# Summing two weight blocks in HBM by an accumulating DMA, and seven products in place of eight in seven more granules

## The chip, the cores and the metric

The kernel runs on one core of a Trainium2 chip. The time is device microseconds of one execution, and the time before is the median of three runs. The core has five engines with a queue each, which go through their instructions in order and wait for each other by semaphores: PE (matrix products), DVE (element-wise), ACT (element-wise and functions), POOL (element-wise, and DMAs of its own) and SP, which here only issues DMAs. The transfers themselves run on 16 DMA engines that all queues share. Weights lie in HBM; PE reads SBUF and writes PSUM, which has eight banks of 128 x 512 f32 words.

## The reference

One decoder layer for 256 tokens of width 2048. The input is normalized and multiplied with one wide matrix, the result is cut into nine parts, two token mixers run side by side, and their outputs are merged by gates and projected:

```python
h = rms_norm(x, norm_g)
q, k, v, z_a, u_b, v_b, z_b, g_a, g_b = jnp.split(h @ w_in, cuts, axis=-1)
q = rms_norm(q.reshape(B, S, N_ATT_HEADS, HEAD_DIM), q_norm_g)
k = rms_norm(k.reshape(B, S, N_ATT_HEADS, HEAD_DIM), k_norm_g)
att = moba_attention(q, k, v)          # causal here: 256 tokens are one block
y_a = (att * jax.nn.silu(z_a)) @ w_proj_a
sgu = spatial_gating(jax.nn.gelu(u_b), jax.nn.gelu(v_b), sgu_norm_g, w_s, b_s)
y_b = (sgu * jax.nn.silu(z_b)) @ w_proj_b
merged = jax.nn.sigmoid(g_a) * y_a + jax.nn.sigmoid(g_b) * y_b
return x + merged @ w_out
```

q, k, v, z_a, u_b, v_b and z_b are 1024 columns wide, g_a and g_b 2048 each. All inputs are f32. The host may lay the inputs out anew; it does no arithmetic.

## The kernel before, in words

*Granules.* The weights are 120 granules of 128 x 2048 words (1 MB), in the order in which they are used: `schedule()` (L50). A "quad" granule holds four 128 x 512 blocks W12, W11, W22, W21, in this order: two blocks of 128 input features (a pair, `kp`, 0 to 7) by two blocks of 512 output columns. Eight pairs make a stage. The stages are q, k, v, za, vb, ub, zb, then four gate blocks g0 to g3, each followed by four "proj" granules of the two projections, then two output blocks. The order of the pairs within a stage is written out by hand (L43 to L46).

*Three matmuls per product.* A product in f32 is split: each operand is cut into a high part (a cast to fp32r) and a low part (the difference), and low x high, high x high and high x low are added (`three`, L285). ACT makes the high parts of the weights, DVE the low parts.

*Eight products or seven.* A direct granule is eight products of a 128 x 128 block of x with a 128 x 512 block of weights, 24 matmuls (`direct`, L294). Some quad granules use seven products instead (`seven`, L308), after Winograd's form of Strassen's method: 21 matmuls. They need sums of weight blocks, T0 = W12 + W11, T1 = W12 + W22, T2 = T0 + W22, T3 = T2 + W21, and four forms of x that are made once (`four_forms`, L269). `strassen(i)` (L105) says which granules: pairs 0 to 3 of every stage but q, and pair 4 of the gate blocks, 52 in all. Three of the seven products go straight into the output banks `L`, the other four into the banks `E`; after the last seven-product granule of a stage `early` (L333) combines `E`, and `final` (L350) adds `L`. The next stage swaps `E` and `L`. The forms of pair 4 are made by `forms_4`, and `halves_4` puts their two parts in a piece of the tiles of x that only q's direct granules read.

*What DVE and ACT do per granule* is in `split` (L128). For a direct granule, one cast and one difference, 2048 wide. For a seven-product granule: the sums T0 and T1 in one instruction (L143, 1024 wide), T2 (L145) and T3 (L146), into a tile `t` that takes one of the five slots of `raw`; a cast and a difference of the three blocks that are used as they are (L152, L155, 1536 wide, `whp`, `wlp`); and two casts and two differences of the four sums (L154, L157, 1024 wide, `th`, `tl`).

*Order.* The loop at L640 goes over the granules. In step i it emits the load of granule i + 3, the split of granule i + 2, the matmuls of granule i, and then what `at(...)` (L569 to L615) put behind that granule: norms, transposes, attention, the functions. For DVE and ACT this order is kept up to granule 8 (`ordered`, L617); behind it a planner orders each engine's queue by its own estimate of times. The slots limit how far the splits run ahead: the tags `wh` and `wl` have three, `whp` three, `wlp` two, `raw` five. A load waits for its slot of `raw` on SP's queue, and what is behind it there waits too. POOL has a few masks and constants, and the power in `rsqrt` (L244) for the norms of q, k and vb.

Of the kernel before, what the change touches and what calls it, by code (L numbers as in the profile page):

```python
# [20 lines left out]
P = 128  # L21
S = 256
# [45 lines left out]
def hybrid_layer_kernel(  # L68
# [18 lines left out]
    psum = ctx.enter_context(tc.tile_pool(name="psum", bufs=1, space=bass.MemoryType.PSUM))  # L87

# [13 lines left out]

    raw, wh, wl, th, tl = {}, {}, {}, {}, {}

    def strassen(i):  # L105
# [22 lines left out]
    def split(i, pieces=1, js=None):  # L128
# [3 lines left out]
        if not strassen(i):  # L132
# [4 lines left out]
            for j in js or range(pieces):  # L137
# [3 lines left out]
        t = wpool.tile([P, WORDS], F32, tag="raw", bufs=5, name=f"t{i}")  # L141
        two = t[:, 0:2 * B].rearrange("p (a n) -> p a n", a=2)
        nc.vector.tensor_tensor(two, r[:, B:3 * B].rearrange("p (a n) -> p a n", a=2),  # L143
                                r[:, None, 0:B].to_broadcast([P, 2, B]), op=ALU.add)
        nc.vector.tensor_tensor(t[:, 2 * B:3 * B], t[:, 0:B], r[:, 2 * B:3 * B], op=ALU.add)  # L145
        nc.vector.tensor_tensor(t[:, 3 * B:], t[:, 2 * B:3 * B], r[:, 3 * B:], op=ALU.add)  # L146
        wh[i] = wpool.tile([P, 3 * B], F32R, tag="whp", bufs=3, name=f"whp{i}")
        wl[i] = wpool.tile([P, 3 * B], F32R, tag="wlp", bufs=2, name=f"wlp{i}")
        th[i] = wpool.tile([P, WORDS], F32R, tag="wh", bufs=3, name=f"th{i}")
        tl[i] = wpool.tile([P, WORDS], F32R, tag="wl", bufs=3, name=f"tl{i}")  # L150
        a, b = slice(0, 2 * B), slice(2 * B, WORDS)
        nc.scalar.copy(wh[i], r[:, B:])  # L152
        for sl in (a, b):
            nc.scalar.copy(th[i][:, sl], t[:, sl])  # L154
        nc.vector.tensor_tensor(wl[i], r[:, B:], f(wh[i]), op=ALU.subtract)  # L155
        for sl in (a, b):
# [604 lines left out]
```

## Time and profile before

| what | us |
|---|---|
| median of three runs (660.52 to 661.25) | 660.79 |
| the profiled execution | 660.26 |
| its span, first to last instruction | 658.5 |
| PE busy, 2980 matmuls and transposes | 650.4 |
| DVE busy, 606 instructions | 606.3 |
| ACT busy, 564 instructions | 427.8 |
| POOL busy, 26 instructions | 25.3 |
| time of the DMA engines taken by SP's queue | 55.4% |

The span counts what the profiler recorded on the engines; the execution's own time is a little longer. A busy time says how long an engine had something in work, so two engines can both be busy nearly all the time; which of them sets the pace is seen only where one waits for the other. "PEld" is the loading of the stationary operand, which overlaps the matmuls. In a timeline a row is the start in us from the span's beginning, the length in us, the engine, the line, the operation and its tiles, and in brackets the idle time before it with what ended it.

### The profile page before, as it was taken

Reading aid. Unit: us, or ns where it says so; the run is one execution under the profiler, and the core shown is the slowest. Engines: PE = TensorE matmul, PEld = TensorE weight load, DVE = VectorE, ACT = ScalarE, POOL = GpSimd, SP = SyncE. Lnnn points to the kernel's source line nnn. Section 1 sums busy time; section 2 is a strip of 40 time slices with the busy share of each in tenths; the row PEclk is TensorE's granted clock in tenths of the full one; section 3 lists DMA queues with packets and bytes.
Section 4 is the critical chain, followed back from the end, with each engine's and each line's share of the span. In section 5 each row is a group of like instructions: output and inputs, shape, how many; then the busy total and the mean of one; then the engine's idle time right before and its main releaser. Section 6 shows DMA issues by size and latency. Waiting matters only on the chain.

```text
span 658.5 us, 7820 instructions
## 1 busy us (share of the span) xinstructions
PE 650.4 (99%) x2980; PEld 538.7 (82%) x2980; DVE 606.3 (92%) x606; ACT 427.8 (65%) x564; POOL 25.3 (4%) x26
## 2 busy tenths in 40 slices
PE   8999999999999999999999999999999999999997
PEld 5888887888888888888888888888888888888886
DVE  5879997999999799999999999899799979998995
ACT  7889779658886589675655755556474546746360
POOL 1002203000000003000000000000000000000000
PEclk9999999999999999999999999999999999999999
DMA  8975643652664456456449436834755483557641
GB/s 312 420 311 209 261 153 129 255 193 86 236 222 161 163 188 219 165 192 230 153 159 351 137 127 264 302 130 190 266 183 192 137 319 130 189 190 282 198 153 64
DMA packets 22213, 135.32 MB, mean 205 GB/s; under 512 B 2464, under 2 KB 3104, under 8 KB 7072
## 3 DMA queue, kind: packets, MB, share of 16 engines
q1 hardware_dynamic: 21024, 132.73, 55.4%
q10 hardware_dynamic: 1152, 2.10, 0.9%
q8 instruction: 23, 0.38, 0.2%
q14 instruction: 14, 0.11, 0.1%
HBM read 132.72 MB, written 2.10 MB: 205 GB/s over the span
## 4 chain that ended last, share of the span: by engine, by line
PE 93%; DVE 3%; POOL 1%; DMA 1%; issue 1%; ACT 0%; SPq 0%; DVEq 0%
PE acc_g L290 16%; PE y L290 13%; PE acc_out L290 9%; PE seven_g L290 8%; PE acc_q L290 6%; PE acc_vb L290 5%; PE acc_za L290 5%; PE acc_ub L290 5%; PE acc_zb L290 5%; PE acc_k L290 4%; PE seven_out L290 3%; PE acc_v L290 2%; PE seven_vb L290 2%; PE seven_zb L290 2%; PE seven_ub L290 2%; PE seven_za L290 2%
## 5 line engine op out<-in xcount | busy, mean ns | idle before, releaser
L126 DVE TENSOR_TENSOR wl<-raw,wh 128x2048 fp32r<-128x2048 f32 (+2 forms) x76 | 156.2, 2062 | 27.7 <-ACT wh L125 27.3
L154 ACT CAST th<-t 128x1024 fp32r<-128x1024 f32 x104 | 107.7, 1055 | 102.0 <-DVE t L146 35.3
L125 ACT CAST wh<-raw 128x2048 fp32r<-128x2048 f32 (+2 forms) x76 | 130.9, 1730 | 60.2 <-issue 25.3
L157 DVE TENSOR_TENSOR tl<-t,th 128x1024 fp32r<-128x1024 f32 x104 | 125.2, 1222 | 2.9 <-ACT th L154 2.9
L155 DVE TENSOR_TENSOR wlp<-raw,whp 128x1536 fp32r<-128x1536 f32 x52 | 91.0, 1750 | 1.2 <-ACT whp L152 1.2
L152 ACT CAST whp<-raw 128x1536 fp32r<-128x1536 f32 x52 | 76.8, 1482 | 23.6 <-DMA raw<-in_w 21.5
L143 DVE TENSOR_TENSOR t<-raw 128x1024 f32<-128x1024 f32 x52 | 63.3, 1218 | 1.8 <-DMA raw<-in_w 1.5
L290 PE MATMUL acc_g<-wh,xul 128*128 128x512 f32 x96 | 37.3, 389 | 0.0
L290 PE MATMUL acc_g<-wh,xuh 128*128 128x512 f32 x96 | 37.3, 389 | 0.0
L290 PE MATMUL acc_g<-wl,xuh 128*128 128x512 f32 x96 | 37.3, 389 | 0.0
L145 DVE TENSOR_TENSOR t<-t,raw 128x512 f32<-128x512 f32 x52 | 36.0, 691 | 0.2
L146 DVE TENSOR_TENSOR t<-t,raw 128x512 f32<-128x512 f32 x52 | 35.6, 685 | 0.4
L290 PE MATMUL acc_q<-wh,xuh 128*128 128x512 f32 x64 | 25.0, 391 | 1.2 <-ACT wh L125 1.2
L290 PE MATMUL acc_q<-wl,xuh 128*128 128x512 f32 x64 | 25.2, 395 | 0.3 <-DVE wl L126 0.2
L290 PE MATMUL y<-wh,zbl 128*128 128x512 f32 x64 | 25.1, 392 | 0.0
L290 PE MATMUL y<-wh,zal 128*128 128x512 f32 x64 | 25.0, 390 | 0.0
L290 PE MATMUL acc_q<-wh,xul 128*128 128x512 f32 x64 | 24.9, 390 | 0.0
L290 PE MATMUL acc_out<-wh,mh 128*128 128x512 f32 x64 | 24.9, 389 | 0.0
L290 PE MATMUL acc_out<-wl,mh 128*128 128x512 f32 x64 | 24.9, 389 | 0.0
L290 PE MATMUL y<-wl,zah 128*128 128x512 f32 x64 | 24.9, 389 | 0.0
L290 PE MATMUL y<-wh,zbh 128*128 128x512 f32 x64 | 24.9, 389 | 0.0
L290 PE MATMUL y<-wl,zbh 128*128 128x512 f32 x64 | 24.9, 389 | 0.0
(496 smaller groups left out, 1582.2 us busy)
## 6 DMA issues: line engine op xcount, KB each, us to landing
raw<-in_w SPq DMA_DIRECT2D x116, 1024.0 KB, 4.8
raw<-in_w SPq DMA_DIRECT2D x7, 512.0 KB, 8.1
xnat<-in_x SPq DMA_DIRECT2D x2, 1024.0 KB, 16.0
xres<-in_x ACTq DMA_DIRECT2D x8, 256.0 KB, 3.9
out<-out_c SPq DMA_DIRECT2D x5, 256.0 KB, 2.5
xt<-in_xT SPq DMA_DIRECT2D x2, 512.0 KB, 8.2
xt<-in_xT SPq DMA_DIRECT2D x3, 256.0 KB, 9.0
raw<-in_w SPq DMA_DIRECT2D x2, 256.0 KB, 4.3
```

The source lines that it names most:

```text
L125: nc.scalar.copy(h, r)
L126: nc.vector.tensor_tensor(l, r, f(h), op=ALU.subtract)
L143: nc.vector.tensor_tensor(two, r[:, B:3 * B].rearrange("p (a n) -> p a n", a=2), r[:, None, 0:B].to_broadcast([P, 2, B]), op=ALU.add)
L145: nc.vector.tensor_tensor(t[:, 2 * B:3 * B], t[:, 0:B], r[:, 2 * B:3 * B], op=ALU.add)
L146: nc.vector.tensor_tensor(t[:, 3 * B:], t[:, 2 * B:3 * B], r[:, 3 * B:], op=ALU.add)
L152: nc.scalar.copy(wh[i], r[:, B:])
L154: nc.scalar.copy(th[i][:, sl], t[:, sl])
L155: nc.vector.tensor_tensor(wl[i], r[:, B:], f(wh[i]), op=ALU.subtract)
L157: nc.vector.tensor_tensor(tl[i][:, sl], t[:, sl], f(th[i][:, sl]), op=ALU.subtract)
L290: nc.tensor.matmul(acc, a, b, start=(start and n == 0), stop=(stop and n == 2))
```

## The change

*The first sum is made in HBM.* A ring of six HBM tiles of 128 x 512 words is added. For each seven-product granule, SP copies its first block (W12) from the weights into a tile of the ring (`pre_copy`, emitted eight granules ahead), and POOL issues a DMA that adds the second block (W11) onto it (`pre_sum`, six granules ahead). The load of such a granule (three ahead, as before) is then two DMAs: the sum from the ring into the first 512 words of `raw`, and the other three blocks as they are.

*Fewer sums on DVE.* `raw` now begins with W12 + W11. T2 is its sum with W22, T1 is T2 - W11, T3 is T2 + W21: three instructions of 512. `raw` as a whole is cut into `wh` and `wl` (2048 wide), the three new sums into `th` and `tl` (1536 wide), with one cast and one difference each.

*More granules with seven products.* Pair 4 in k, v, vb and zb, and pair 5 in g1, g2 and g3: 59 instead of 52. The forms of pair 5 (`forms_5`) have tiles of their own; `halves_4` moves from granule 20 to granule 8. The orders of the pairs change in these stages.

*Slots and order.* `raw` has four slots, `t` one of its own (1536 wide), `wh` and `wl` three for all granules, `th` three, `tl` two. SP's and POOL's queues are now in the order of the program throughout. The masking of the mixing weights (`causal_mix`) moves from stage vb to stage ub; the tile with x's first piece and the vectors is released early, after the vectors are copied.

```diff
+LATE = (5, 6, 0, 1, 2, 3, 4, 7)
+GATE6 = (6, 0, 1, 2, 3, 4, 5, 7)
+FIVE = ("k", "v", "vb", "zb", "g")
+SIX = (1, 2, 3)
...
-        quad(name, 0, MIXED)
+        quad(name, 0, {"k": GATE, "v": LATE, "vb": LATE, "zb": LATE}.get(name, MIXED))
     for c in range(4):
-        quad("g", c, GATE)
+        quad("g", c, GATE6 if c in SIX else GATE)
...
+    queues = {mybir.EngineType.SP, mybir.EngineType.Pool}
+    ctx.enter_context(tc.manual_schedule(engines=queues))
+    ring = [dram.tile([P, B], F32, tag=f"ring{n}", name=f"ring{n}") for n in range(6)]
...
-        return G[i][3] in SK or (G[i][1] == "g" and G[i][3] == 4)
+        name, c, kp = G[i][1:4]
+        return kp in SK or (name in FIVE and kp == 4) or (name == "g" and c in SIX and kp == 5)
...
-        raw[i] = wpool.tile([P, WORDS], F32, tag="raw", bufs=5, name=f"raw{i}")
+        raw[i] = wpool.tile([P, WORDS], F32, tag="raw", bufs=4, name=f"raw{i}")
+
+    def pre_copy(i):
+        if i < NG and strassen(i):
+            pre[i] = ring[len(pre) % len(ring)]
+            nc.sync.dma_start(pre[i], w[i, :, 0:B])
+
+    def pre_sum(i):
+        if i in pre:
+            nc.gpsimd.dma_start(pre[i], w[i, :, B:2 * B], accum_op=ALU.add)
...
+        if i in pre:
+            nc.sync.dma_start(raw[i][:, 0:B], pre[i])
+            load_piece(i, B, WORDS)
+            return
...
-        t = wpool.tile([P, WORDS], F32, tag="raw", bufs=5, name=f"t{i}")
...
+        t = wpool.tile([P, 3 * B], F32, tag="t", bufs=1, name=f"t{i}")
+        wh[i] = wpool.tile([P, WORDS], F32R, tag="wh", bufs=3, name=f"wh{i}")
+        wl[i] = wpool.tile([P, WORDS], F32R, tag="wl", bufs=3, name=f"wl{i}")
+        th[i] = wpool.tile([P, 3 * B], F32R, tag="th", bufs=3, name=f"th{i}")
+        tl[i] = wpool.tile([P, 3 * B], F32R, tag="tl", bufs=2, name=f"tl{i}")
+        T1, T2, T3 = (t[:, a * B:(a + 1) * B] for a in range(3))
+        nc.scalar.copy(wh[i], r)
+        nc.vector.tensor_tensor(T2, r[:, 0:B], r[:, 2 * B:3 * B], op=ALU.add)
+        nc.vector.tensor_tensor(T1, T2, r[:, B:2 * B], op=ALU.subtract)
+        nc.vector.tensor_tensor(T3, T2, r[:, 3 * B:], op=ALU.add)
+        nc.scalar.copy(th[i], t)
+        nc.vector.tensor_tensor(wl[i], r, f(wh[i]), op=ALU.subtract)
+        nc.vector.tensor_tensor(tl[i], t, f(th[i]), op=ALU.subtract)
...
+    def forms_5():
+        Fs = u("F5").rearrange("p (a k t) -> p a k t", a=4, t=P)
+        four_forms(Fs, xt[1][:, 2:4, :])
+        nc.scalar.copy(F5h, Fs)
+        nc.vector.tensor_tensor(F5l, Fs, f(F5h), op=ALU.subtract)
...
+    at(i0 + 4, lambda: nc.scalar.copy(vec, vec0))
     at(i0 + 4, forms_4)
+    at(i0 + 4, forms_5)
...
-    at(i0 + 20, halves_4)
+    at(i0 + 8, halves_4)
...
     at(i0 + 0, turn_z, "za", None)
+    at(i0 + 0, causal_mix)
...
         if i:
             load(i + 3)
+        if i >= 1:
+            pre_copy(i + 8)
+            pre_sum(i + 6)
         split(i + 2, 2 if i < 2 else 1)
```

More of the change, by code (lines that the diff above doesn't have):

```diff
@@ L87, in hybrid_layer_kernel @@
     psum = ctx.enter_context(tc.tile_pool(name="psum", bufs=1, space=bass.MemoryType.PSUM))
+    dram = ctx.enter_context(tc.tile_pool(name="dram", bufs=1, space=bass.MemoryType.DRAM))
     def slot(dtype, name):
@@ L140, in split @@
             return
-        t = wpool.tile([P, WORDS], F32, tag="raw", bufs=5, name=f"t{i}")
[L142 to L156, printed above, removed]
-            nc.vector.tensor_tensor(tl[i][:, sl], t[:, sl], f(th[i][:, sl]), op=ALU.subtract)
+        t = wpool.tile([P, 3 * B], F32, tag="t", bufs=1, name=f"t{i}")
[11 more added lines that the diff above has]
+        nc.vector.tensor_tensor(tl[i], t, f(th[i]), op=ALU.subtract)
     X = {}
@@ L162, in heads @@
         return ap.rearrange("p (h d) -> p h d", d=P)
-    xv = const.tile([P, NVEC + S], F32, name="xv")
-    vec = xv[:, 0:NVEC]
+    xv = u("xv")
+    vec0 = xv[:, 0:NVEC]
+    vec = const.tile([P, NVEC], F32, name="vec")
     xt = [slot(F32, f"xt{i}").rearrange("p (k t) -> p k t", t=S) for i in range(2)]
@@ L175, in hybrid_layer_kernel @@
     new_raw(0)
-    nc.sync.dma_start(xv, xT[:, 0:NVEC + S])
+    nc.sync.dma_start(xv[:, 0:NVEC + S], xT[:, 0:NVEC + S])
     load_piece(0, 0, B)
@@ L207, in split_x @@
         for j in js or range(2):
-            src = xv[:, NVEC:] if kp + j == 0 else xt[i][:, a + j, :]
-            nc.scalar.activation(xt[i][:, a + j, :], src, AF.Copy, scale=vec[:, 2 * kp + j:2 * kp + j + 1])
+            src = xv[:, NVEC:NVEC + S] if kp + j == 0 else xt[i][:, a + j, :]
+            nc.scalar.activation(xt[i][:, a + j, :], src, AF.Copy, scale=vec0[:, 2 * kp + j:2 * kp + j + 1])
         sl = slice(a + js[0], a + js[0] + 1) if js else slice(a, a + 2)
@@ L217, in hybrid_layer_kernel @@
     mhalf = const.tile([P, 8], F32, name="mhalf")
-    nc.gpsimd.memset(mhalf, -0.5)
-    ninf = const.tile([P, 1], F32, name="ninf")
+    nc.gpsimd.memset(mhalf[:, 0:4], -0.5)
+    ninf = mhalf[:, 4:5]
     nc.gpsimd.memset(ninf, NEG_INF)
@@ L233, in load_mix, with causal_mix @@
             nc.sync.dma_start(t, wsT[:, 4 * c:4 * c + 4, :])
+        nc.sync.dma_start(gain, bass.AP(tensor=sg.tensor, offset=sg.offset, ap=[[0, P], [1, P]]))
+    def causal_mix():
+        for c in range(2):
+            t = heads(X["ws"][c])
             nc.gpsimd.affine_select(out=t, in_=t, pattern=[[0, 4], [1, P]], base=0,
                                     channel_multiplier=-1, compare_op=ALU.is_ge, fill=0.0)
-        nc.sync.dma_start(gain, bass.AP(tensor=sg.tensor, offset=sg.offset, ap=[[0, P], [1, P]]))
     rstd = const.tile([P, 2], F32, name="rstd")
@@ L258, in forms_4 @@
         X["F4"] = Fs[:, :, 0]
+    F5h, F5l = (const.tile([P, B], F32R, name=n).rearrange("p (a k t) -> p a k t", a=4, t=P) for n in ("F5h", "F5l"))
+    def forms_5():
[3 more added lines that the diff above has]
+        nc.vector.tensor_tensor(F5l, Fs, f(F5h), op=ALU.subtract)
     def halves_4():
@@ L317, in Fm @@
                 return spare(hs[0])[:, n], spare(ls[0])[:, n]
+            if kp == 5:
+                return F5h[:, n, 0], F5l[:, n, 0]
             return Fh[:, n, kp, :], Fl[:, n, kp, :]
         def W(b):
-            o = (BLK[b] - 1) * B
+            o = BLK[b] * B
             return wh[i][:, o:o + B], wl[i][:, o:o + B]
         def T(n):
-            return th[i][:, n * B:(n + 1) * B], tl[i][:, n * B:(n + 1) * B]
+            if n == 0:
+                return W("12")
+            return th[i][:, (n - 1) * B:n * B], tl[i][:, (n - 1) * B:n * B]
         for acc, (hi, lo), (bh, bl) in ((L[0], A(1, 0), W("21")), (L[1], Fm(3), W("22")), (E[0], A(0, 0), W("11")),
@@ L617, in hybrid_layer_kernel @@
     ordered = ExitStack()
-    ordered.enter_context(tc.manual_schedule(engines={mybir.EngineType.Activation, mybir.EngineType.DVE}))
+    ordered.enter_context(tc.manual_schedule(engines=queues | {mybir.EngineType.Activation, mybir.EngineType.DVE}))
     split_x(0, [0])
@@ L660, in hybrid_layer_kernel @@
             if strassen(i):
-                last = 4 if name == "g" else SK[-1]
+                last = SK[-1] if name not in FIVE else 5 if name == "g" and c in SIX else 4
                 f8 = "m" if name == "out" else "x"
```

1 line of the change is left out of this document (added).

## The prediction

> **What bounds the kernel now.** I read the page's first part, then the chain of waits, then single stretches. The first part says which engine has no room:
>
> ```profile
> PE 650.4 (99%) x2980; PEld 538.7 (82%) x2980; DVE 606.3 (92%) x606; ACT 427.8 (65%) x564; POOL 25.3 (4%) x26
> ```
>
> PE is busy in 650.4 of the span's 658.5 us, DVE in 606.3. So two engines have to be followed: PE, and DVE, which makes PE's operands. The chain of waits, in order of time (start, length, what), is PE from 13.74 us on, apart from one detour through DVE between 90 and 116 us:
>
> ```profile
> 13.74 37.24 PE acc_q L290 x163
> ...
> 113.39 2.29 DVE wl L126
> ...
> 136.01 5.44 PE acc_za L290 x24
> ...
> 654.57 0.42 DVE out_c L348
> ```
>
> The 24 matmuls of a direct granule (eight products of three) take 5.44 us, so one takes 5.44/24 = 0.2267 us, and a seven-product granule (21 matmuls) 4.76 us. PE's own list shows the one stall:
>
> ```profile
> 115.73 0.51 PE L290 MATMUL acc_v<-wl,xuh 128*128 128x512 f32 x1 [1.32 <-DVE wl L126]
> ```
>
> PE stood 1.32 us there, waiting for wl of v's fifth granule (pair 6). DVE was not behind by work: just before that wl it had made wlp of the sixth granule (pair 2), not yet needed, and it finished that granule's last tl long before PE asked:
>
> ```profile
> 111.72 1.75 DVE L155 TENSOR_TENSOR wlp<-raw,whp 128x1536 fp32r<-128x1536 f32 x1
> 113.39 2.28 DVE L126 TENSOR_TENSOR wl<-raw,wh 128x2048 fp32r<-128x2048 f32 x1
> 115.59 2.35 DVE L157 TENSOR_TENSOR tl<-t,th 128x1024 fp32r<-128x1024 f32 x2
> ...
> 122.41 2.72 PE seven_v L290 x12
> ```
>
> The stall is one of order. The last row is from the chain: PE took that granule's W11 product at 122.41 us, and tl was complete at 115.59 + 2.35 = 117.94 us.
>
> **How far ahead DVE is** decides whether fewer products help. By stretch (us, then busy time of PE, PEld, DVE, ACT, POOL), for the stages k, v, zb and the second gate block:
>
> ```profile
> 51.00:90.40 39.40, 39.40 (x175) 32.63 (x175) 36.87 (x36) 32.20 (x68) 7.64 (x4) 1.00 0.54 197
> 90.40:136.00 45.60, 44.28 (x204) 36.55 (x203) 41.49 (x46) 34.76 (x70) 5.72 (x4) 1.00 0.52 191
> 275.60:319.90 44.30, 44.30 (x213) 37.31 (x212) 44.04 (x45) 29.66 (x39) 0.00 (x0) 1.00 0.56 191
> 383.60:423.70 40.10, 40.10 (x178) 33.20 (x178) 38.34 (x37) 21.48 (x18) 0.00 (x0) 1.00 0.61 231
> ```
>
> DVE has 2.5, 4.1, 0.3 and 1.8 us left. That looks like no room, but the buffers let the splits run at most two granules ahead, and busy time that keeps a full lead is not lateness. Two places show the lead. The first row of each pair is DVE's last tl of a granule, the second the stretch of PE that consumes it:
>
> ```profile
> 317.51 1.22 DVE L157 TENSOR_TENSOR tl<-t,th 128x1024 fp32r<-128x1024 f32 x1
> 326.73 2.72 PE seven_g L290 x12
> ...
> 412.75 1.22 DVE L157 TENSOR_TENSOR tl<-t,th 128x1024 fp32r<-128x1024 f32 x1
> 414.86 2.72 PE seven_g L290 x12
> 415.30 2.29 DVE L126 TENSOR_TENSOR wl<-raw,wh 128x2048 fp32r<-128x2048 f32 x1 [1.33 <-ACT wh L125]
> ```
>
> At the end of zb the tl of gate block 0's second granule is done at 318.73, 8.0 us before PE starts that granule's twelve E products. In gate block 1 the tightest one, the last granule of the run, is done at 413.97; its second slice is used by the third sum, 11 matmuls in (2.5 us): at 417.35, so 3.4 us to spare. The last row shows DVE even waiting 1.33 us for ACT there.
>
> **The change, part by part.**
>
> *Products.* Seven granules go from eight products to seven: k, v, vb, zb (pair 4) and gate blocks 1 to 3 (pair 5). Each product is three matmuls, so 21 matmuls go: 21 x 0.2267 = 4.76 us. PE's records should fall from 2980 to 2959.
>
> *DVE per seven-product granule.* From starts of neighbouring DVE instructions (records overlap by some 0.08 us, so starts count, not lengths):
>
> ```profile
> 51.37 2.28 DVE L126 TENSOR_TENSOR wl<-raw,wh 128x2048 fp32r<-128x2048 f32 x1
> 53.57 0.68 DVE L146 TENSOR_TENSOR t<-t,raw 128x512 f32<-128x512 f32 x1
> ...
> 57.58 0.68 DVE L145 TENSOR_TENSOR t<-t,raw 128x512 f32<-128x512 f32 x1
> 58.18 1.75 DVE L155 TENSOR_TENSOR wlp<-raw,whp 128x1536 fp32r<-128x1536 f32 x1
> 59.85 0.68 DVE L146 TENSOR_TENSOR t<-t,raw 128x512 f32<-128x512 f32 x1
> 60.45 1.21 DVE L157 TENSOR_TENSOR tl<-t,th 128x1024 fp32r<-128x1024 f32 x1
> 61.59 0.16 DVE L243 TENSOR_SCALAR ms<-ss 128x4 f32<-128x4 f32 x1
> ```
>
> 2048 wide takes 2.20 us, 512 wide 0.60, 1536 wide 1.67, 1024 wide 1.14. Before: 1.14 + 0.60 + 0.60 for the sums, 1.67 for wlp, 2 x 1.14 for tl = 6.29 us. After: three sums of 0.60, wl 2.20, tl 1.67 = 5.67 us. So 0.62 us less in each of the 52 old ones, and 5.67 - 2.20 = 3.47 us more in each of the seven new ones: -32.2 + 24.3 = -7.9 us over the kernel. ACT changes from 1.48 + 2 x 1.06 to 1.91 + 1.48 us:
>
> ```profile
> L125 ACT CAST wh<-raw 128x2048 fp32r<-128x2048 f32 x64 | 122.4, 1912 | 58.3 <-issue 25.3 <-PE acc_g L290 24.1 <-PE acc_out L290 3.9
> L154 ACT CAST th<-t 128x1024 fp32r<-128x1024 f32 x104 | 107.7, 1055 | 102.0 <-DVE t L146 35.3 <-issue 11.7 <-PE y L290 10.5
> L152 ACT CAST whp<-raw 128x1536 fp32r<-128x1536 f32 x52 | 76.8, 1482 | 23.6 <-DMA raw<-in_w 21.5 <-PE seven_vb L290 1.9
> ```
>
> That is 0.2 us less per granule by these means, off the path.
>
> *DVE per stage.* k, v, vb and zb each: four old ones -2.48, one new +3.47, so +1.0 us, while PE has 0.68 less. za and ub: -2.48. Gate blocks 1 to 3: +0.4. So k and v together are 3.4 us tighter, zb 1.7, each later gate block 1.1 us; za, ub, gate block 0 and both output blocks are looser. The longest run of seven-product granules becomes five (v, vb, zb) or six (gate); inside it DVE loses 5.67 - 4.76 = 0.91 us per granule, 5.5 us over six, and the direct granules and projections around it give it back. For the gate: before, five and one direct took DVE 5 x 6.29 + 2.20 = 33.7 us against PE's 29.2; after, 34.0 against 28.6: 1.1 us of the 3.4 goes, and 0.7 more because tl is now one instruction, which the second sum waits for. Some 1.6 us stay, so no stall. In zb the 8.0 us less 1.7 stay. In v, a single tl of pair 2 would be wanted eight matmuls after 122.41, at 124.2, 6.3 us after 117.94; without PE's own 1.3 us of lateness that is 5.0. Of it k and v take 3.4, and each later granule of the run 0.91: at the edge of zero. Cost of all that: from -1.3 (the stall of order falls away) to +3.4 us (nothing in k and v is absorbed). I take +0.8, nearer the lower end, since what rows show is lead; the 1.32 us stall thus stays, and grows a little or finds a companion.
>
> *Forms of the sixth pair.* Four small DVE forms, one ACT cast, one DVE difference in q:
>
> ```profile
> L273 DVE TENSOR_TENSOR F<-xt 128x128 f32<-128x128 f32 x1 | 0.3, 284 | 0.0
> L262 DVE TENSOR_TENSOR xul<-F,xuh 128x512 fp32r<-128x512 f32 x1 | 0.7, 693 | 0.7 <-ACT xuh L261 0.7
> 13.70:51.00 37.30, 37.26 (x164) 30.89 (x165) 29.48 (x29) 32.36 (x36) 0.71 (x1) 1.00 0.92 372
> ```
>
> 4 x 0.28 + 0.69 = 1.8 us, and halves_4 (0.69) moves into q's end. DVE has 37.30 - 29.48 = 7.8 us free there, so 0; without that cover up to 2.5 us at k's second granule.
>
> *The ring.* For each of 59 granules: an SP copy of 256 KB from HBM to HBM, a POOL-issued accumulating DMA of 256 KB, and the 1 MB load cut into 256 KB (behind the sum) and 768 KB. No row shows an HBM-to-HBM or an accumulating transfer; the nearest are:
>
> ```profile
> out<-out_c SPq DMA_DIRECT2D x5, 256.0 KB, 2.5
> ws<-in_wsT SPq DMA_DIRECT2D x2, 256.0 KB, 5.6
> raw<-in_w SPq DMA_DIRECT2D x116, 1024.0 KB, 4.8
> L244 POOL TENSOR_TENSOR rs<-ms,mhalf 128x4 f32<-128x4 f32 x12 | 19.9, 1673 | 101.3 <-DVE ms L243 101.3
> ...
> 61.82 7.64 POOL L244 TENSOR_TENSOR rs<-ms,mhalf 128x4 f32<-128x4 f32 x4 [18.03 <-DVE ms L243]
> ```
>
> 256 KB land in 2.5 to 5.6 us. For the accumulate, which reads two and writes one, I bound 2.5 to 11 us (twice the slow row) and take 5; POOL's issue I bound by 0 and its dearest small operation (1.7 us). Copy, sum and load are then some 4 + 5 + 5 = 14 us. The copy is issued eight granules ahead in the program, the load three, so five granules (24 us) lie between: hidden. SP is one ordered queue: behind a load that waits for the sum stand the next loads, copies and the mixing weights. POOL is ordered too: a sum stands behind the rs powers of q, k and vb and the masking of ws. The powers of q (last row) have their place at k's second granule, which PE starts at 13.74 + 37.24 + 5.44 = 56.4 us, and end at 69.5: 2.7 granules late. The first sum behind them is for a granule nine after that place, whose load SP reaches about four after it; so one granule remains, and two more before its split. Behind POOL's waiting sum stand only later sums and rs. Raw has four slots rather than five, but sums no longer take any: a load now always waits for the split four granules back, before for one three back in mixed runs. That is 0. DMA engines were full in q:
>
> ```profile
> 35.00:40.00 5.00, 5.00 (x24) 4.14 (x23) 2.60 (x2) 3.98 (x5) 0.00 (x0) 1.00 1.02 423
> 45.00:55.00 10.00, 10.00 (x46) 8.29 (x45) 10.00 (x7) 9.02 (x10) 0.00 (x0) 1.00 0.31 109
> ```
>
> At 423 GB/s a 0.262 MB pass is 0.62 us; five granules of k add five copies and five sums of two passes, 9.3 us, and from 45 to 55 us there are 10 x (1 - 0.31) = 6.9 us free. The rest, 2.4 us, is within the two granules of lead. 0, at most 2.4.
>
> *Other edits.* xv to a recycled tile, the 26-column copy, masking moved, memsets merged: single instructions under 1.2 us on engines that wait anyway; 0. The order of the first loads before 13.7 us is unchanged.
>
> *Sum.* 658.5 - 4.76 + 0.8 = 654.5 us of span. The profiled execution took 660.26 us, 1.76 more than its span: 656.3. The median of the runs, 660.79, is 0.53 above that execution: **656.8 us**.
>
> **Rivals.**
> 1. *DVE takes part of it back.* k and v are not absorbed (+3.4, not 0.8): 659.4. For: 41.49 of 45.60 busy in v, and ACT's k sums sit in the same stretch. Against: tl done 4.5 us before 122.41, and the lead in zb and the gate.
> 2. *One t buffer (slower).* The next granule's sums may not start until this one's th and tl are done, where before they ran ahead in raw's slots. Place: every seven-product granule where ACT is late with th. If DVE idles x us per granule, k, v, vb and zb lose 5x each; k has 39.40 - 0.68 - 36.87 - 1.0 = 0.8 us of room, v by the same working 2.4, a gate run 1.6 in six granules. It costs from x = 0.8 / 5 = 0.16 on and eats the gain at 0.45 (k 1.45, gates 3 x 1.1); at x = 0.6 k loses 2.2, v 0.6 and the gates 3 x 2.0, 8.8 in all, less the 4.76: 664.8. For: ACT's th idles 35.3 us for t in the row above. Against: that is ACT's idle time, not DVE's, and wl (2.20) now covers th (1.48).
> 3. *The accumulate is slow (slower).* With p us per sum, five in k's 38.7 us bind from p = 7.7. At p = 9 k takes 45 rather than 38.7 us (+6.3), zb 45 rather than 43.6 (+1.4), less 4.8: 663.7. For: POOL's 128x4 power took 1.67 us on average and 0.71 beside an idle DVE:
>
> ```profile
> 43.08 0.71 POOL L244 TENSOR_TENSOR rstd<-ms,mhalf 128x2 f32<-128x2 f32 x1 [39.96 <-DVE ms L243]
> ```
>
> Beside these rows: the Trainium skill, "SBUF — State Buffer", section "SBUF: two separate sides", warns that the descriptors of a POOL-issued DMA are written through a port which some DVE operations lock; the next section, "A bandwidth-pool intuition that's wrong (but worth ruling out)", has such a DMA of 620 ns taking 3100 ns. The power rows go the same way; no row here shows a descriptor being written. By the page, an estimate, 59 x 3.1 = 183 us would be spent on a POOL that is 4% busy, and the sum above would stay as it is; the same page's "Who interferes with whom" gives tensor_tensor, which is nearly all that DVE does here, no mode that locks both ports.
> 4. *The products go and the stall of order too*: 660.79 - 4.76 - 1.3 = 654.7.
>
> **How the numbers follow.** Forecast 0.55 (own range 655.3 to 658.4); rival 4 0.12; rival 1 0.15, half of it past 659.47; rival 2 0.11; rival 3 0.07. A change under 0.2% (1.32 us: 659.47 to 662.11) can't be told from none here. Faster: 0.55 + 0.12 + 0.07 = 0.74; same: 0.08 and 0.02 of rival 2: 0.10; slower 0.16. Range: 654.3 to 661.5, which leaves out some 0.03 below and 0.16 above.
>
> **What would show it.** PE x2959, with busy time near 645.6; DVE near 600; a sum of 1536 behind one th in every seven-product granule; POOL DMA issues x59, landing in under 8 us; no wait of ACT's wh or DVE's sums on raw over 2 us; SP's waits on the ring short. Wrong: a new PE wait on tl or wl in v, zb or a six-run above 1 us each (rivals 1, 2), loads that start right after a sum lands (3), or a PE count unchanged.

## The result and the profile after

The changed kernel took 667.75 us (median of four runs, 665.38 to 668.79) against 660.81 us before (660.52 to 661.25, the same chip): a ratio of 1.010, 95% interval 1.0069 to 1.013. It is slower by 7 us; the forecast was 656.8, its range ended at 661.5. So 11 us had to be found.

The page of the changed kernel: busy times, the two largest DMA queues (packets, MB, share of the 16 engines' time), and landing times of the transfers (KB each, median us from issue to landing).

```profile
span 667.1 us, 8042 instructions
PE 653.7 (98%) x2959; PEld 533.4 (80%) x2959; DVE 601.8 (90%) x587; ACT 432.3 (65%) x521; POOL 73.2 (11%) x85
q1 hardware_dynamic: 38016, 148.21, 60.2%
q0 software_dynamic: 8496, 15.47, 15.6%
...
raw<-in_w SPq DMA_DIRECT2D x57, 1024.0 KB, 7.3
raw<-in_w SPq DMA_DIRECT2D x59, 768.0 KB, 6.7
ring<-in_w SPq DMA_DIRECT2D x59, 256.0 KB, 7.9
ring<-in_w POOLq DMA_DIRECT2D x59, 256.0 KB, 7.6
raw<-ring SPq DMA_DIRECT2D x59, 256.0 KB, 4.6
```

Two sums of the forecast came out: PE has 2959 products, VectorE 601.8 us (forecast 600). But PE's busy time did not fall, and a plain 1 MB load, which landed in 4.8 us before, now takes 7.3 (medians). The chain of waits (start, length, what), nearly all PE from 13.74 us on before, now starts with a load of q, passes through ScalarE and VectorE into k, and meets loads again in the gate blocks:

```profile
23.24 16.86 DMA raw<-in_w
...
81.37 1.76 DVE tl L177
83.18 1.62 PE seven_k L323 x4
...
352.60 7.32 DMA raw<-in_w
```

VectorE's list in that part of k shows the order that the planner wrote (L172 to L174 are the sums of T, L176 and L177 the remainders wl and tl of a seven-product granule, L150 the wl of a direct one):

```profile
75.56 0.68 DVE L172 TENSOR_TENSOR t<-raw 128x512 f32<-128x512 f32 x1
...
79.16 2.29 DVE L176 TENSOR_TENSOR wl<-raw,wh 128x2048 fp32r<-128x2048 f32 x1 [1.59 <-ACT wh L171]
81.37 1.75 DVE L177 TENSOR_TENSOR tl<-t,th 128x1536 fp32r<-128x1536 f32 x1
83.04 2.29 DVE L150 TENSOR_TENSOR wl<-raw,wh 128x2048 fp32r<-128x2048 f32 x1
85.24 0.69 DVE L172 TENSOR_TENSOR t<-raw 128x512 f32<-128x512 f32 x1
85.84 2.29 DVE L150 TENSOR_TENSOR wl<-raw,wh 128x2048 fp32r<-128x2048 f32 x1
...
88.64 0.69 DVE L174 TENSOR_TENSOR t<-t,raw 128x512 f32<-128x512 f32 x1
91.14 2.29 DVE L150 TENSOR_TENSOR wl<-raw,wh 128x2048 fp32r<-128x2048 f32 x1 [1.81 <-ACT wh L149]
93.35 1.75 DVE L177 TENSOR_TENSOR tl<-t,th 128x1536 fp32r<-128x1536 f32 x1
```

The tl at 81.37 is that of granule 13. Only behind it may granule 14's sums start (one t buffer), and between it and granule 14's tl at 93.35 stand three wl of direct granules (15, 16, 17), which PE wants later. PE's list shows what late operands cost:

```profile
80.55 0.50 PE L323 MATMUL seven_k<-th,Flx 128*128 128x512 f32 x1 [0.67 <-ACT th L175]
83.18 0.50 PE L323 MATMUL seven_k<-tl,Fhx 128*128 128x512 f32 x1 [1.89 <-DVE tl L177]
83.51 0.43 PE L323 MATMUL seven_k<-th,Flx 128*128 128x512 f32 x1
83.74 0.63 PE L323 MATMUL seven_k<-th,Fhx 128*128 128x512 f32 x1
...
86.73 0.59 PE L323 MATMUL acc_k<-wl,xuh 128*128 128x512 f32 x1
87.15 0.39 PE L323 MATMUL acc_k<-wh,xul 128*128 128x512 f32 x1
```

PE waits 0.67 and 1.89 us, and then, from 83.74 to 87.15, its eight starts lie 0.427 us apart in place of 0.227: 1.6 us more. So there are three suspects. Theory A: the one t buffer with the order that follows from it. Theory B: the ring's transfers. Theory C: 59 granules are too much for VectorE in any order.

### The profile page after: what moved, and what is told of

Its sections match the earlier page's. It is cut to its first block, busy times and chain, and to the rows that moved or that the text cites. A ratio compares the mean times of both kernels' runs of the same rounds, so it can differ in the third digit from the quotient of the medians.

```text
span 667.1 us, 8042 instructions
## 1 busy us (share of the span) xinstructions
PE 653.7 (98%) x2959; PEld 533.4 (80%) x2959; DVE 601.8 (90%) x587; ACT 432.3 (65%) x521; POOL 73.2 (11%) x85
## 3 DMA queue, kind: packets, MB, share of 16 engines
q0 software_dynamic: 8496, 15.47, 15.6%
## 4 chain that ended last, share of the span: by engine, by line
PE 67%; DVE 13%; ACT 8%; DMA 6%; issue 4%; POOL 1%; SPq 0%; DVEq 0%; ACTq 0%; POOLq 0%
PE y L323 13%; PE acc_g L323 11%; PE seven_g L323 6%; DMA raw<-in_w 6%; PE acc_za L323 5%; PE acc_ub L323 4%; PE acc_zb L323 4%; PE acc_vb L323 4%; DVE wl L176 3%; ACT wh L149 3%; PE acc_out L323 3%; DVE wl L150 3%; DVE tl L177 3%; PE acc_v L323 2%; PE seven_zb L323 2%
## 5 line engine op out<-in xcount | busy, mean ns | idle before, releaser
L150 DVE TENSOR_TENSOR wl<-raw,wh 128x2048 fp32r<-128x2048 f32 (+2 forms) x69 | 140.2, 2039 | 21.3 <-ACT wh L149 21.3
L149 ACT CAST wh<-raw 128x2048 fp32r<-128x2048 f32 (+2 forms) x69 | 117.4, 1713 | 60.5 <-PE acc_g L323 19.5
L171 ACT CAST wh<-raw 128x2048 fp32r<-128x2048 f32 x59 | 112.6, 1914 | 61.5 <-issue 12.8
L176 DVE TENSOR_TENSOR wl<-raw,wh 128x2048 fp32r<-128x2048 f32 x59 | 134.8, 2286 | 6.6 <-ACT wh L171 6.4
L175 ACT CAST th<-t 128x1536 fp32r<-128x1536 f32 x59 | 87.5, 1483 | 59.5 <-DVE t L174 58.1
L177 DVE TENSOR_TENSOR tl<-t,th 128x1536 fp32r<-128x1536 f32 x59 | 103.9, 1760 | 5.2 <-ACT th L175 5.2
L134 POOL DMA_DIRECT2D ring<-in_w x59 | 49.0, 882 | 456.0 <-DMA ring<-in_w 438.4
L172 DVE TENSOR_TENSOR t<-raw 128x512 f32<-128x512 f32 x59 | 40.9, 693 | 10.0 <-DMA raw<-in_w 9.4
L173 DVE TENSOR_TENSOR t<-t,raw 128x512 f32<-128x512 f32 x59 | 40.6, 687 | 0.9
L174 DVE TENSOR_TENSOR t<-t,raw 128x512 f32<-128x512 f32 x59 | 40.4, 684 | 0.0
L323 PE MATMUL acc_out<-wh,ml 128*128 128x512 f32 x72 | 28.0, 391 | 0.0
```

The costliest lines, as they stand in the source:

```text
L134: nc.gpsimd.dma_start(pre[i], w[i, :, B:2 * B], accum_op=ALU.add)
L149: nc.scalar.copy(h, r)
L150: nc.vector.tensor_tensor(l, r, f(h), op=ALU.subtract)
L171: nc.scalar.copy(wh[i], r)
L172: nc.vector.tensor_tensor(T2, r[:, 0:B], r[:, 2 * B:3 * B], op=ALU.add)
L173: nc.vector.tensor_tensor(T1, T2, r[:, B:2 * B], op=ALU.subtract)
```

## The experiments

Times are medians, with the 95% interval of the ratio to the kernel before, which took 660.4 to 660.7 us beside each of them. "No ring" kernels leave out the addition of block 12 to block 11.

**Which of the two: the ring or the buffer?** First the ring away (a granule comes by one 1 MB load):

```diff
-        if i < NG and strassen(i):
+        if False:
             pre[i] = ring[len(pre) % len(ring)]
```

> The changed kernel without the ring: no copy into an HBM tile, no accumulating sum; a seven-product granule comes with one plain 1 MB load. Left out of the computation: the addition of block 12 to block 11 that the sum made. Products, splits and the order of TensorE are those of the changed kernel. Theory A (one t buffer with VectorE's written order: weight remainders of later granules stand ahead of the sums and remainders of T, so T products wait) leaves that in place: 664 to 668 us, and TensorE still waits for tl in k, v and the gate blocks. Theory B (the ring's transfers: loads that land at 7 us in place of 5, SyncE's queue, q's full DMA engines) says most of the 12 us goes: 655 to 658, and k's start is back at 50.8 us. Theory C (59 granules of seven products are too many for VectorE whatever the order) says 663 to 668. If A and B share the loss, about 661.

Measured: 660.79 us, ratio 0.9999 (0.999 to 1.0009). The ring costs 7.0 us (667.75 - 660.79), and not by another order of work: PE goes through the same order in both kernels, VectorE and ScalarE through the same but for two places each. The stall shown above goes with the ring too, though it looks like theory A: VectorE's order in k is the same here, and the same tl of granule 13, behind a like wait for ScalarE (1.62 us), comes 3.4 us earlier, and PE does not wait for it:

```profile
77.97 1.75 DVE L177 TENSOR_TENSOR tl<-t,th 128x1536 fp32r<-128x1536 f32 x1
```

But 21 products fewer bring nothing either. Then, still without the ring, t with two buffers in the same bytes:

```diff
-        t = wpool.tile([P, 3 * B], F32, tag="t", bufs=1, name=f"t{i}")
+        t = wpool.tile([P, 3 * B], F32, tag="t", bufs=2, name=f"t{i}")
...
-        th[i] = wpool.tile([P, 3 * B], F32R, tag="th", bufs=3, name=f"th{i}")
+        th[i] = wpool.tile([P, 3 * B], F32R, tag="th", bufs=2, name=f"th{i}")
```

> No ring (the addition of block 12 to block 11 is left out), 59 granules, t with two buffers and th with two in place of three, so the same bytes. The planner then lays the sums of the next granule before the T remainder of this one. Theory A (the one t buffer is why 21 products fewer bring nothing without the ring): the waits for tl and th and the short gaps behind them (about 3.5 us over those of the kernel before) go, 656.0 to 658.5. If VectorE's work for 59 granules is too much whatever the buffers (C): 659.5 to 661.5. If two th buffers are too few: above 661.

Measured: 657.24 us, ratio 0.9949 (0.9934 to 0.9964). Pages of the two, without the ring with one and with two t buffers:

```profile
PE 651.3 (99%) x2959; PEld 534.5 (81%) x2959; DVE 602.1 (91%) x587; ACT 433.3 (66%) x521; POOL 23.3 (4%) x26
raw<-in_w SPq DMA_DIRECT2D x116, 1024.0 KB, 4.9
```

```profile
PE 647.9 (99%) x2959; PEld 535.9 (82%) x2959; DVE 600.6 (92%) x587; ACT 432.8 (66%) x521; POOL 23.5 (4%) x26
DVE t L172 <- DMA raw<-in_w: 2.2, 4, 0.9
```

VectorE's work is the same (602.1 and 600.6 us), so theory C falls: with room for the order, 59 granules fit. The one buffer, against two of t and one fewer of th, costs 3.5 us. Much of it can be read from PE's starts after 14 us. With one buffer 31 products start 0.03 to 0.15 us late, at or just behind a product whose th, tl or wl had nearly always only just been finished, some 3 us in all; with two buffers it is 9 products and 0.8 us, in the kernel before 2 and 0.2 us. Loads land as before the change (4.9 us). The second row of the second page, from the waits, is kept for later: VectorE's sums waited for loads 2.2 us in all.

With the old 52 granules, with and without the ring:

```diff
-FIVE = ("k", "v", "vb", "zb", "g")
-SIX = (1, 2, 3)
+FIVE = ("g",)
+SIX = ()
```

> The changed kernel with the old choice of granules and their old order within a stage: 52 seven-product granules, so 2980 products, with the ring, the new split and four raw slots. It shows what the ring and the new split cost by themselves. Theory A: fewer runs of five and six, so the T products are late less often: 660 to 664. Theory B: 52 of 59 rings remain, the loss of 12 us shrinks to 10 and 4.8 us of products come back: 668 to 671. Theory C: 658 to 661.

> The changed kernel without the ring (the addition of block 12 to block 11 is left out) and with the old 52 granules in their old order: only the new split, the t tile of one buffer and the four raw slots are left of the change. Beside the run with the ring and 52 granules (672.2 us) it gives the ring's price with the granules held fixed; beside the run without the ring and with 59 granules (660.8) it gives what seven more granules are worth. If the ring alone costs what it cost with 59 granules (667 to 668 against 660.8, about 6.5 us), this is 664 to 667, and the new split itself costs 4 to 6. If the split and the buffers cost nothing with 52 granules, this is 659.5 to 661.5, the ring's price is 11 us there, and seven more granules without the ring are worth nothing.

Measured: 672.23 us (ratio 1.0142 to 1.0192) with the ring, 661.36 (1.0001 to 1.002) without. So the new split, its one buffer and four raw slots are nearly free with 52 granules (0.7 us); the ring costs 10.9 us there. All three theories had missed the 672: none had the ring dearer with fewer granules.

**VectorE in granule order.** If the order is at fault, does the plain one cure it? From the first seven-product granule on, each granule's part on VectorE was put behind that of the granule before (`lastv` holds the last VectorE instruction of each split, `split_one` is the old body of `split`); the second run has no ring as well:

```diff
         r = raw[i]
+        with tc.issue_after(lastv[-1]) if lastv else ExitStack():
+            split_one(i, r, pieces, js)
```

> The changed kernel with one edge of order: VectorE's part of each granule's split stands behind that of the granule before it, so sums of T, remainders and T remainders go granule by granule, and no remainder of a later direct granule goes ahead of a T remainder. Same transfers, same products. Theory A: the lost time in k to v and in blocks g1 to g3 (about 5 and 3 x 1 us, and part of g0) comes back: 655 to 660, with tl of granule 74 done before TensorE wants it. Theory B: no change beyond 2 us, 665 to 668. Theory C: VectorE still takes as long, 664 to 668.

> Both edits together: no ring (the addition of block 12 to block 11 is left out) and VectorE's split in granule order. Theories A and B together: the sum of the two gains, down to the forecast without any stall, 653 to 657. Theory C: still over 661, because VectorE's work per granule is the same.

Measured: 725.09 us with the ring (ratio 1.0953 to 1.1004) and 711.79 us without (1.0758 to 1.079): theory A's forecast of a gain was wrong by over 50 us in both. VectorE's waits in the run without the ring (us in total, times, longest):

```profile
DVE tl L185 <- ACT th L183: 71.4, 44, 3.3
```

With one t buffer and no other work to fill in, VectorE stands 71.4/44 = 1.6 us for ScalarE's th in each of 44 granules. The planner's order had avoided that (5.9 us in 7 waits without the ring) by putting later wl in the gap, and paid with the late products counted above. Neither order helps; without the ring, the second buffer does.

**What of the ring costs?** Nobody waits for the ring: every copy and sum is made, but each granule comes by a plain 1 MB load and the sums are not used.

```diff
-        if i in pre:
-            nc.sync.dma_start(raw[i][:, 0:B], pre[i])
-            load_piece(i, B, WORDS)
-            return
```

> The changed kernel with every copy and every accumulating sum of the ring still made, but nobody waits for them: each seven-product granule comes with one plain 1 MB load, and no ring tile is read (so the addition of block 12 to block 11 is made and thrown away). Traffic theory (the copies and sums fill DMA engines and make loads land late): 665 to 668, loads of 1 MB land at a median near 7 us. Waiting theory (the load waits in SyncE's queue for the sum, and holds up the loads behind it): back to the run without the ring, 660 to 662.

Measured: 669.56 us (1.0098 to 1.0162), as slow as the changed kernel. It is traffic, not the waiting. Then its halves, again not used: copies alone (`pre_sum` left empty), sums alone (a copy only where `len(pre) <= len(ring)`, so six), and the second of these with plain writes by the same queue:

```diff
-            nc.gpsimd.dma_start(pre[i], w[i, :, B:2 * B], accum_op=ALU.add)
+            nc.gpsimd.dma_start(pre[i], w[i, :, B:2 * B])
```

> As the run whose ring nobody waits for, but with the 59 copies alone: no accumulating sum is issued (nor is block 12 added to block 11 anywhere). 15.5 MB read and written less the sums' share. If the copies are half of the traffic's price: 664 to 666, loads of 1 MB landing near 6 us. If the accumulating sums carry it (POOL's queue was busy 16% of the engines for 15.5 MB): 661 to 662.5. If the copies carry it: 667 to 669.

> The other half: 59 accumulating sums by POOL, and six copies in place of 59 (the first one into each ring tile); nobody reads the ring, each granule comes with one 1 MB load (block 12 isn't added to block 11 in what is used). Half of the price: 664 to 666. The sums carry it: 667 to 669. The copies carry it: 661 to 662.5. In either case the two runs' prices over 660.8 should add up to about the 8.8 us of both together; less than that in sum would say that the loads' spare time swallows a part.

> As the run with 59 sums by GpSimd and six copies (666.8 us), with the same 59 transfers of 256 KB from GpSimd's queue as plain writes, not accumulations; nobody reads the ring (block 12 isn't added to block 11). If the accumulation in the DMA engines is what costs: 660.5 to 662.5, as with 59 copies from SyncE's queue (661.5), and 1 MB loads land near 4.9 us. If the way by GpSimd's queue costs: 665 to 668, loads near 6.1 us.

Measured: 661.50 us with the copies (1.0007 to 1.0026), 666.84 with the sums (1.0078 to 1.0126), 663.44 with plain writes (1.0024 to 1.0053). Over the 660.79 without any: 0.7, 6.1 and 2.7 us. The copies and the sums, run separately, add up to 6.8 us; run together they cost 8.8 (669.56). The plain writes lie between the two cases of their expectation. The runs with sums and with plain writes have exactly the orders of PE, VectorE and ScalarE of the run without the ring, so traffic alone differs. GpSimd's queue and the landing of 1 MB loads, of the copies, the sums and the plain writes:

```profile
raw<-in_w SPq DMA_DIRECT2D x116, 1024.0 KB, 4.9
```

```profile
q0 software_dynamic: 8496, 15.47, 14.1%
raw<-in_w SPq DMA_DIRECT2D x116, 1024.0 KB, 6.1
```

```profile
q0 software_dynamic: 4720, 15.47, 7.3%
raw<-in_w SPq DMA_DIRECT2D x116, 1024.0 KB, 5.0
```

The same 15.47 MB hold the 16 engines for 14.1% of the span as accumulations and 7.3% as writes: 0.141 x 16 x 665.2 / 59 = 25.4 us of engine time per sum against 13.1. So the accumulation itself takes the larger part (3.4 of 6.1 us), and the loads pay: 6.1 us in place of 4.9 and 5.0. One reserve: with no copy to wait for, the sums and the plain writes of these two runs were all issued by 357 and 302 us (606 in the changed kernel), so they are priced in the first half of the kernel alone.

Where it is paid can be seen by two stretches, the second half of q and k with v (length, busy time of PE, PEld, DVE, ACT, POOL, granted clock, DMA share, GB/s), without the ring and with the sums:

```profile
20.00:51.00 31.00, 31.00 (x139) 25.66 (x138) 26.02 (x31) 24.13 (x26) 0.71 (x1) 1.00 0.91 366
51.00:137.00 86.00, 85.55 (x382) 69.51 (x381) 78.98 (x77) 69.46 (x132) 11.25 (x8) 1.00 0.54 197
```

```profile
20.00:51.00 31.00, 31.00 (x139) 25.66 (x138) 22.65 (x27) 23.54 (x25) 5.07 (x6) 1.00 1.02 392
51.00:137.00 86.00, 82.92 (x360) 66.43 (x359) 76.85 (x76) 68.23 (x132) 22.87 (x22) 0.98 0.78 232
```

The engines of the DMA, 0.91 busy in q, are full (1.02) with the sums; the load of k's first granule lands at 43.2 us and not at 38.8. PE loses nothing in q. In k and v it gets through 360 products and not 382, 22 x 0.2267 = 5.0 us of work: 85.55 - 82.92 = 2.6 us more it stands, and most of the rest is a stretch at half the clock (the granted clock is 0.98 in the mean). Spatial v starts at 189.8 us, not at 183.9. From there to the start of the output blocks both take the same 386.7 us.

So the ring was kept out of k alone (whose granules then lack the addition):

```diff
-        if i < NG and strassen(i):
+        if 16 <= i < NG and strassen(i):
```

> The changed kernel with the ring only from v on: k's five seven-product granules come with one plain load, and block 12 isn't added to block 11 in them. 54 of 59 copies and sums are left, and they begin later. If the sums hurt through q, where the engines of the DMA are already full, and through k's lead (granule 8 then lands at 39 us, not 43): 662 to 664, k to v 3 to 4 us shorter. If the price is spread over all stages: 666.5 to 667.5.

Measured: 664.75 us (1.0052 to 1.0081), 3.0 less; spatial v starts at 183.4 us. Five of 59 rings carry 3.0 of the 7 us. The other 4 lie late: gate block 0 starts at 318.8 us in both, and from there to the output blocks it takes 255.6 us here against 251.8 without a ring. The changed kernel's own trace divides alike: k takes 43.0 us and not 38.2, the gate blocks 2.9 us more.

A fifth raw slot, for the room of the sixth pair's forms:

```diff
-SIX = (1, 2, 3)
+SIX = ()
...
-        raw[i] = wpool.tile([P, WORDS], F32, tag="raw", bufs=4, name=f"raw{i}")
+        raw[i] = wpool.tile([P, WORDS], F32, tag="raw", bufs=5, name=f"raw{i}")
...
-        th[i] = wpool.tile([P, 3 * B], F32R, tag="th", bufs=3, name=f"th{i}")
+        th[i] = wpool.tile([P, 3 * B], F32R, tag="th", bufs=2, name=f"th{i}")
```

> The changed kernel, ring included, without the sixth pair (56 granules, 2968 products), and the room of its forms spent on a fifth raw slot, with th in two buffers. Between the runs with the ring and 52 (672.2) and 59 granules (667.7) 56 would give about 669.6 if slots play no part. Theory: the ring's later landings hurt because four raw slots leave them no room (a slot is taken from the load's issue to VectorE's last read); a fifth slot gives 5 us more lead, more than the 2.5 us that loads land later: 660 to 664. If it is the T products' order alone, or TensorE is disturbed in another way: 667 to 671.

Measured: 666.87 us (1.0073 to 1.0107). Against the 669.6 worked out for 56 granules that is some 3 us at most, not the 6 to 9 that the theory asked: the slots are not where most of the ring's price comes from. (This run has one th buffer fewer, and the 669.6 is a straight line between 52 and 59 granules.)

**Two t buffers with the ring**, by the edit of t and th above; the second run with the edit of the ring that nobody waits for.

> The whole changed kernel, ring included, with t in two buffers and th in two in place of three. Theory A and B side by side: the one buffer's part (3 to 4 us) comes back and the ring's part (6 to 7) stays, 662 to 665. If late loads and late T products are one loss (a load that lands late hits only where the order had used up the lead), more comes back than without the ring: 658 to 661. If the ring is all that counts: 666 to 668.

> t and th with two buffers each, all copies and sums made, nobody waits for them (plain 1 MB loads, the sums thrown away); orders of TensorE and VectorE as with two t buffers and the ring in use (677.0). Waiting theory for the 677: 661 to 666, and no wait of 9 us of VectorE for a raw tile at 271 us. Traffic alone: 673 to 678.

> The whole changed kernel with t and th in two buffers, and the ring begun two granules earlier: copy ten ahead, sum eight ahead, eight ring tiles. The sums then stand in GpSimd's queue ahead of the square roots of the spatial v, which wait for ScalarE. Waiting theory: zb's 8 us come back, 665 to 669 (the sums' traffic in q and k stays). Traffic alone: 675 to 679.

The last one's edit is below; its copies begin with granule 11, so granules 9 and 10 come without the addition.

```diff
-            pre_copy(i + 8)
-            pre_sum(i + 6)
+            pre_copy(i + 10)
+            pre_sum(i + 8)
```

Measured: 677.02 us (1.023 to 1.026), with nobody waiting 674.07 (1.0176 to 1.0215), with early sums 670.63 (1.014 to 1.0167). The second buffer, worth 3.5 us without the ring, costs 9 with it (677.02 - 667.75 = 9.3), against all three cases of the expectation. VectorE's waits for a raw tile at the first sum of T, in the same three kernels (the second runs the changed kernel's transfers with shifted line numbers):

```profile
DVE t L172 <- DMA raw<-in_w: 29.4, 10, 9.4
```

```profile
DVE t L168 <- DMA raw<-in_w: 23.5, 11, 5.0
```

```profile
DVE t L172 <- DMA raw<-in_w: 22.3, 7, 5.0
```

Without the ring this row was 2.2 us. The orders of PE and VectorE are those of the run with two t buffers and no ring, but for three places on VectorE. They put the sums of the next granule ahead of older work, which is right where a load lands in 4.8 us. Where it lands later, VectorE stands still at the head of its queue. The longest wait is that of zb's first seven-product granule, and GpSimd's list (ahead) and VectorE's (behind) show how it comes:

```profile
253.98 9.55 POOL L269 TENSOR_TENSOR rs<-ms,mhalf 128x4 f32<-128x4 f32 x4 [25.87 <-DVE ms L268]
```

```profile
280.56 0.69 DVE L172 TENSOR_TENSOR t<-raw 128x512 f32<-128x512 f32 x1 [9.41 <-DMA raw<-in_w]
```

The sum's place is behind the powers of spatial v's norm (L269), which wait 25.87 us for VectorE and end at 263.5 us. That wait is a part only: with nobody waiting the row still has 23.5 us. The waiting theory had put that run at 661 to 666; it falls for the larger part. The early sums gain 6.4 us and end between their two cases; the run also moves the traffic, so it doesn't price the waiting alone.

**Can a whole computation keep the gain?** Three more kernels leave nothing out. First k's additions by VectorE, the ring from v on with early sums, two t buffers; then the addition by GpSimd in the raw tile, with no ring, two t buffers and GpSimd's queue left to the planner; then the kernel before with the fifth pair in k, v, spatial v and zb:

```diff
+        if i not in pre:
+            nc.vector.tensor_tensor(r[:, 0:B], r[:, 0:B], r[:, B:2 * B], op=ALU.add)
         nc.scalar.copy(wh[i], r)
```

```diff
+        nc.gpsimd.tensor_tensor(r[:, 0:B], r[:, 0:B], r[:, B:2 * B], op=ALU.add)
         nc.scalar.copy(wh[i], r)
```

```diff
-        return G[i][3] in SK or (G[i][1] == "g" and G[i][3] == 4)
+        return G[i][3] in SK or (G[i][1] in FIVE and G[i][3] == 4)
```

> The whole computation: t and th in two buffers, the ring from v on with the copy ten and the sum eight granules ahead, and in k block 12 added to block 11 by VectorE in the raw tile (five times 0.69 us more there). If q and k carry the sums' price and the late sum carries the wait: 658 to 661, about the kernel before. If the price is spread: 664 to 670.

> No ring; block 12 is added to block 11 in the raw tile itself by GpSimd, one 128x512 addition per seven-product granule, so the whole computation is done; t and th in two buffers each, 59 granules. GpSimd isn't held to program order. No run so far shows such an addition on GpSimd: VectorE takes 0.69 us for it, and GpSimd's selection over 128x512 stands in the rows at some microseconds. If the addition (1 to 3 us) fits in the 5 us that a granule waits for its turn: 657 to 659, faster than the kernel before by 0.3 to 0.5%. If it makes the wl's late in the runs of five and six granules, or slows VectorE where both read the raw tile: 661 to 668.

> The kernel before, whole computation, no ring, old split and its t tile from the raw slots, with the fifth pair by seven products in k, v, spatial v and zb too (56 granules, the changed kernel's orders in these stages). 12 products fewer are 2.7 us; VectorE gets 4 x 4.0 = 16 us more (6.29 us in place of 2.29 a granule), to 622. If the leads hold: 657.5 to 658.5. If VectorE takes it back in k and v, where its spare time was least: 660 to 664.

Measured: 663.07 us (1.0027 to 1.0054), 689.59 (1.0424 to 1.0472) and 669.61 (1.0091 to 1.0142). None beats the kernel before, and the last two are slower than either case of their expectations. The rows of GpSimd's addition and of VectorE's page with it:

```profile
PE 657.1 (96%) x2959; PEld 536.5 (78%) x2959; DVE 635.5 (93%) x587; ACT 433.0 (63%) x521; POOL 153.6 (22%) x85
...
L171 POOL TENSOR_TENSOR raw<-raw 128x512 f32<-128x512 f32 x59 | 126.0, 2137 | 492.4 <-DMA raw<-in_w 435.7 <-issue 33.0 <-DVE tl L178 5.8
```

GpSimd takes 2.14 us for one, and VectorE's same work went from 600.6 to 635.5 us. This agrees with the Trainium skill, "SBUF — State Buffer", section "Who interferes with whom": a VectorE instruction with two inputs in SBUF contends with a GpSimd instruction that reads SBUF. In the last kernel PE waits for VectorE in k, v and zb, among other places:

```profile
PE seven_k L292 <- DVE tl L159: 1.5, 1, 1.5
PE seven_zb L292 <- DVE tl L159: 1.2, 1, 1.2
PE seven_v L292 <- DVE tl L159: 0.9, 1, 0.9
```

That fits theory C for the old split, 6.29 us a granule: the dearer split and the additional granules together leave PE waiting. It isn't shown, since the pairs' order changed with the granules and no run separates the two; two of the six runs took 665 us and four 669 to 670.

## Why the prediction was wrong

The 11 us between forecast and result divide by three runs: 657.24 - 656.8 = 0.4 (no ring, two t buffers), 660.79 - 657.24 = 3.5 (one t buffer), 667.75 - 660.79 = 7.0 (the ring). The division holds in this order alone: with two t buffers the ring costs 677.02 - 657.24 = 19.8 us, and the second buffer then loses 9.3.

- *Products* and *VectorE per granule* held: 2959 products, 601.8 us against 600. Without ring and with two t buffers PE was busy 647.9 us (forecast 645.6), and the time met the forecast to 0.4 us. That confirms these two terms, not the forecast: this kernel has neither the ring nor the one buffer.
- *VectorE per stage*, taken at +0.8 with bounds of -1.3 and +3.4, was mis-sized too: with one buffer it came to 0.8 + 0.4 + 3.5 = 4.7 us, if the 0.4 is put down to it as well, past the upper bound. The step counted work and lead, and said that a granule's sums no longer need a raw slot; it did not ask what VectorE's written order becomes with one t buffer. That question stood in rival 2 with the right place and the wrong form: it priced VectorE standing idle (0.6 us a granule), where the planner filled the gap with other remainders and the products of T came late, by some 0.1 us each. Idle time is what appears in granule order, 1.6 us a granule.
- *The ring* was the failed step. Its chain of copy, sum and load was set at 14 us within 24 us of lead, and was indeed hidden: nobody waiting changes nothing for the better (669.6). The mistake was to ask only how long the ring's own transfers take, and to put what they do to others at 0 (at most 2.4 us in q). It measured 7.0 us. The accumulating sums hold the DMA engines twice as long as plain writes of the same bytes (25.4 and 13.1 us), q's engines were already full, and a 1 MB load lands 2.5 us later at the median. The step also set k's transfers against the time free from 45 to 55 us, where they don't fall: the five copies were issued from 14.6 to 34.8 us and the first two sums at 24.5 and 27.9, and in the kernel before the DMA share from 14 to 35 us was already 1.02. "Within the two granules of lead" fell with that: k's first wl was ready 1.7 us before PE started k, against 5.3 without the ring.
- *Rival 3* had a slow sum, but as a wait with a threshold of 7.7 us; sums landed in 7.6 us at the median, below it, and the loss came all the same. The row of 0.71 us that spoke for it is also of a power half as wide (128x2) as those of 1.67 us.
- *GpSimd's queue*: a sum stood behind the powers of spatial v, as the step said. With one t buffer PE did not feel it (zb took 44.0 us, before 44.4); with two it did.
- *Issue of the sums*: 0.88 us each (row below) and VectorE's busy time unmoved (601.8 and 602.1 us with and without ring). The estimate by the Trainium skill, "SBUF — State Buffer", section "A bandwidth-pool intuition that's wrong (but worth ruling out)", of 3.1 us each and 183 us in all was not met; it was 49.0 us.

```profile
L134 POOL DMA_DIRECT2D ring<-in_w x59 | 49.0, 882 | 456.0 <-DMA ring<-in_w 438.4 <-issue 8.9 <-DVE t L174 8.8
```

- Of what was to show it, two signs came out wrong: VectorE's sums were to wait for raw no longer than 2 us (9.4 us in 3 waits, longest 4.2), and SyncE's waits on the ring were to be short (41.0 us in 14, longest 8.8). These signs were the right ones.

What stays open: why the ring is dearer with 52 granules (10.9 us) than with 59 (7.0). The traces show only where: with 52, k takes 40.8 us with and without the ring, but the stage za takes 3.3 us more, zb 1.9 and the output blocks 5.1. So the price seems to depend on where the transfers fall, but no run separates what decides it. Open is also how much of the 2.7 us of plain writes from GpSimd is due to their coming in bursts.

## What to carry to other kernels

A transfer that nobody waits for still has a price where the DMA engines are busy: before moving arithmetic into DMA, look at the landing time of the loads and at the DMA share of the fullest stretch, and price the kind of transfer by itself. Where a planner writes the order once, a buffer saved or added changes that order: ask what will stand in front of what when one input is late. And take a loss apart in more than one order: the second buffer gained 3.5 us with the ring away and lost 9.3 with it there.

## What was not expected of the hardware

- After a wait TensorE may run at half pace. In the list above, eight products took 0.427 us each after waits of 0.67 and 1.89 us, and the granted clock in that stretch was 0.51:

```profile
83.70:87.20 3.50, 3.50 (x10) 2.68 (x10) 3.50 (x3) 0.40 (x1) 0.00 (x0) 0.51 1.02 274
```

With two t buffers and the ring the same came after one wait of 3.2 us at 120 us. It is not certain: with nobody waiting for that ring, the same wait of 3.2 us was followed by no slow product, nor was one of 2.3 us at 141 us with the ring and 52 granules. The Trainium skill, "TensorE: Matmul & The Clock Gate", section "Part 1: The HAM clock gate (the "warmup" mystery)", gives 426.7 ns for such a product on a cold array and a free-running window of 3.4 us; the pace and the length (8 x 0.427 = 3.4 us) agree, but the waits here were shorter than a whole window. A wait of 1.9 us thus cost 3.5 (1.89 + 1.6).
- A short wait costs PE a second time: the product after the one that waited also starts some 0.1 us late (83.51 and not 83.41 above). Without the ring and with one t buffer 24 products started late so, 2.4 us in all, behind one whose operand had only just been finished; in the kernel before it was 2. Gaps of 0.09 us also follow products of 128 columns (12 in the kernel before, 14 here); these are in both kernels and are no wait.
- In the changed kernel 256 KB copied from HBM to HBM landed at a median of 7.9 us and accumulated at 7.6, beside 1 MB loads of 7.3; in the kernel before such a load took 4.8.
